# Two row blocks per instruction in the inputs of the second mixer of a two-layer decoder trunk

## The chip, the cores and the metric

The kernel runs on one core of one Trainium2 chip. A core has TensorE (PE, the matrix engine, with its weight loads listed as PEld), VectorE (DVE), ScalarE (ACT) and GpSimd (POOL), which run their own instruction queues in order, and DMA queues that move data between the chip's memory (HBM) and the on-chip memory. The metric is the device time of one execution in microseconds (us); lower is better.

## What is computed

The reference is a trunk of two layers on 16 meta tokens and 256 tokens of width 1024, in float32. Layer 0 is a half-step SwiGLU, attention heads beside gated DeltaNet heads, and another half-step SwiGLU; layer 1 is the same with RWKV-7 time mixing in the middle. The change is in the inputs of that time mixing:

```python
def rwkv7_time_mix(h, mu, w_r, w_k, w_v, w0, w1, w2, a0, a1, a2, g1, g2, k_k, k_a, r_k, ...):
    xx = jnp.pad(h, ((0, 0), (1, 0), (0, 0)))[:, :L] - h          # token differences
    xr, xw, xk, xv, xa, xg = [h + xx * mu[i] for i in range(6)]   # six mixes
    r, k, v = xr @ w_r, xk @ w_k, xv @ w_v
    w_log = -jax.nn.softplus(-(w0 + jnp.tanh(xw @ w1) @ w2)) - 0.5
    a = jax.nn.sigmoid(a0 + (xa @ a1) @ a2)
    g = jax.nn.sigmoid(xg @ g1) @ g2
    kk = l2_normalize((k * k_k).reshape(B_, L, H, N))
    k = k * (1 + (a - 1) * k_a)
    decay = jnp.exp(-jnp.exp(w_log))
    y = rwkv7_recurrence(r, decay, k, v, -kk, kk * a)
    ...
```

## The kernel before

Activations lie transposed: a tile of 128 partitions holds one block of 128 of the 1024 rows (`KD` = 8 blocks), and its T = 272 columns are the tokens. A float32 product is made of three passes of rounded halves (`passes`, lines 216 to 218): every operand is split into a rounding (`h`, made by a cast on ScalarE) and a remainder (`l`, a subtraction on VectorE). Weights go the same way as they are used, 512 columns at a time (`split`, lines 209 and 151).

The time mixing's inputs are made in `TimeMix.inputs`. In order: the low-rank products of the decay, the gate and `a` fill five PSUM banks (`pw`, `pg`); `normed(k)` normalizes block k into `hn` (line 1290) and takes the difference to the token before into `xx`, which lies in the room of `t.hT` (line 1291). `stream(i, s)` makes the mixed input of one of the three large products: per block `mixed` writes `hn + xx * mu` into a tile `mix` (line 1296), line 1304 rounds it into `h`, line 1305 subtracts for `l`. There are three streams: `kx` (key, all made first), `vx` (value) and `rx` (receptance). `joined` (lines 1357 to 1363) forms the low-rank results from two PSUM banks and the token before, by way of a tile `before`. `low_rank` makes the sigmoids of the decay (`ar[:, 1, m]`) and of `a` (`kt[:, m]`), line 1396. `decay(m)` works on block m: a scan along the tokens into `cs` (line 1419), two exponentials (1420, 1421), a copy of five columns into `pc` (1422), the product `bt`, an affine step on `kt` (1424) and the product `kt` with `cs`. The two products are on VectorE for blocks 0 to 3 and on GpSimd for blocks 4 to 7 (`t.tt`, line 151).

Tiles come from the pool `ri`: `mix` and `before` share the tag `mix` with three buffers, `cs` has the tag `low` with four. A tile that finds no free buffer waits until the reader of an older one is done.

`beside` drives the rest: it runs the products of a stream, unit by unit, and takes one step of the given side work after every product of three passes:

```python
beside(units((0, 1), 2, self.key), pairs(low_rank(0, 1, 2, 3)), decays(0, 1))
beside(units((2, 3), 2, self.key), decays(2, 3), sent(0), pairs(chain(low_rank(4, 5, 6, 7), gates())), vx)
beside(units((0, 1), 0, self.value), sent(1), spaced(rx))
beside(units((0, 1), 1, self.receptance), decays(4, 5, 6, 7))
```

A unit's result goes through `key`, `value` or `receptance`, which read the decays' results; `sent(g)` starts the small inverses of a pair of blocks, with DMAs to HBM and back. The program text sets priorities, but a planner orders each engine's instructions by when their inputs and buffers are ready; `after` adds orders by hand (sigmoids and exponentials, which need different activation tables, are kept apart). When the stage ends, `first.close()` gives back the pool `ri`, and the recurrence's tiles (pool `rd`) may take that memory. The recurrence then runs beside the rest of the products (`fills`).

Of the kernel before, what the change touches and what calls it, by code (L numbers as in the profile page):

```python
# [10 lines left out]
F32 = mybir.dt.float32  # L11
F32R = mybir.dt.float32r
AF = mybir.ActivationFunctionType
ALU = mybir.AluOpType
PSUM = bass.MemoryType.PSUM

P = 128
D = 1024
KD = D // P
META = 16  # L20
SEQ = 256
T = META + SEQ
# [6 lines left out]
CH = 64  # L29
# [984 lines left out]
class TimeMix:  # L1014
# [264 lines left out]
    def inputs(self, first):  # L1279

        nc, t, V, ri = self.nc, self.t, self.V, self.ri
        DEC = math.exp(-0.5)
        ar, bt, kt = self.ar, self.bt, self.kt
        hn = self.hn

        xx = t.hT
        ka1 = ri.tile([P, KD], F32, name="ka1")

        def normed(k):
            nc.vector.scalar_tensor_tensor(hn[:, k, 1:], t.hT[:, k, :], self.gain_in[:, k:k + 1], r, ALU.mult, ALU.mult)  # L1290
            nc.vector.tensor_tensor(xx[:, k, :], hn[:, k, 0:T], hn[:, k, 1:], ALU.subtract)

        def mixed(i, k):

            a = ri.tile([P, T + 1], F32, name="mix", tag="mix", bufs=3)[:, :T]
            nc.vector.scalar_tensor_tensor(a, xx[:, k, :], V["mu"][:, KD * i + k:KD * i + k + 1], hn[:, k, 1:], ALU.mult, ALU.add)
            return a

        def stream(i, s):

            h, l = self.x[s]
            for k in range(KD):
                a = mixed(i, k)
                nc.scalar.copy(h[:, k, :], a)
                nc.vector.tensor_tensor(l[:, k, :], a, h[:, k, :].bitcast(F32), ALU.subtract)
                yield

        def pairs(x):
            for _ in x:
# [43 lines left out]
        for k in range(KD):  # L1353
            normed(k)

        def joined(out, now, before, rows):

            n = out.shape[0]
            b = ri.tile([P, T + 1], F32, name="before", tag="mix", bufs=3)[:n]
            nc.gpsimd.memset(b[:, 0:1], 0.0)  # L1360
            nc.vector.tensor_tensor(b[:, 1:], before, r[:n], ALU.mult)
            nc.vector.tensor_tensor(out, now, r[rows], ALU.mult)
            nc.vector.tensor_tensor(out, out, b[:, :T], ALU.add)

        kx = stream(2, 2)
        for _ in range(4):
            next(kx)
        nc.scalar.copy(back[:, 0], self.raw2)
        nc.vector.tensor_tensor(back[:, 1], self.raw2, back[:, 0].bitcast(F32), ALU.subtract)
        mid = self.small("mid")  # L1370
        joined(mid, *pw, slice(0, P))
        nc.scalar.activation(mid[0:64], mid[0:64], AF.Tanh)
        nc.scalar.copy(midh, mid)
        nc.vector.tensor_tensor(midl, mid, midh.bitcast(F32), ALU.subtract)
        for _ in range(4):
            next(kx)
        joined(gmid[0], *pg[:2], slice(0, P))
        joined(gmid[1], pg[2][32:], pg[2][:32], slice(32, 64))
        smask = t.tmp.tile([P, T], F32, name="smask", tag="rstd", bufs=1)
        nc.gpsimd.memset(smask, 1.0)  # L1380
# [6 lines left out]
        def after(which):  # L1387
            stack = ExitStack()
            for x in which:
                stack.enter_context(self.tc.issue_after(x.ins))  # L1390
            return stack
# [22 lines left out]
        def decay(m):  # L1414

            with after(self.sigmoids):
                A, S = kt[:, m], ar[:, 1, m]
                cs = self.decay_tile()
                nc.vector.tensor_tensor_scan(cs, smask, S, 0.0, ALU.mult, ALU.add)
                nc.scalar.activation(S, cs, AF.Exp, scale=-DEC)  # L1420
                self.exps.append(nc.scalar.activation(cs, cs, AF.Exp, scale=DEC))
                nc.scalar.copy(self.pc[:, m, :], S[:, META - 1::CH])
                t.tt(m < 4, bt[:, m], A, cs, ALU.mult)
                nc.scalar.activation(A, A, AF.Identity, scale=V["k_a"][:, m:m + 1], bias=ka1[:, m:m + 1])
                t.tt(m < 4, A, A, cs, ALU.mult)

        self.decay_tile = lambda: ri.tile([P, T], F32, name="cs", tag="low", bufs=4)
        def decays(*ms):
            for m in ms:
                decay(m)  # L1430
                yield

        def sent(g):
            yield
# [5 lines left out]
            yield  # L1440

        vx, rx = stream(3, 0), stream(0, 1)
# [4 lines that stand above are left out]
        self.ready = 0  # L1447
        first.close()
# [431 lines left out]
```

## Time and profile before

| | us |
|---|---|
| median of 3 runs | 1305.07 |
| lowest and highest | 1304.49, 1306.56 |
| the profiled execution | 1305.4 |
| its span in the trace | 1303.7 |
| busy: TensorE, weight loads | 1256.5, 1199.9 |
| busy: VectorE, ScalarE, GpSimd | 901.7, 703.8, 103.6 |

The trace is of the profiled execution. Busy time is the sum of an engine's instructions, overlapping parts counted once. In a timeline a row gives an instruction's start, its duration, engine, line, operation, output and inputs, shapes and count; rows with the same text that follow each other are merged (x2), so their duration is that of all of them together. A list of waits gives who waited for whom, total time, times and the longest. [...]

### The profile page before, as it was taken

What the parts mean: (1) busy time and instruction counts of PE and PEld (TensorE: products, weight loads), DVE (VectorE), ACT (ScalarE), POOL (GpSimd) and SP (SyncE); (2) the same over time, 40 slices, a digit from 0 to 9 for tenths busy, and PEclk for the clock granted to TensorE, in tenths of its full rate; (3) what the DMA queues carried; (4) which work ended last, traced back from release to release, by engine and by line L of the source; (5) the groups of instructions that cost most, each with busy time, mean ns of one, the idle gap of its engine ahead of it and who ended that gap; (6) DMA issues with size and microseconds to landing.
All of it is one profiled execution on the core that took longest, in us unless ns stands there. A gap on an engine that the chain in (4) does not pass through costs nothing.

```text
span 1303.7 us, 28476 instructions
## 1 busy us (share of the span) xinstructions
PE 1256.5 (96%) x11425; PEld 1199.9 (92%) x11425; DVE 901.7 (69%) x1941; ACT 703.8 (54%) x1524; POOL 103.6 (8%) x189
## 2 busy tenths in 40 slices
PE   8999999899999999999999999978999998999997
PEld 8999999788977999999999999967898888999987
DVE  6666666979565866666777766889666677866654
ACT  5555554774455755555555555476444444555553
POOL 2000012002100100000000001103122011000001
PEclk8999999899989999999999999986999999999999
DMA  6545555434112545545656555413432331555652
GB/s 199 188 158 172 167 171 153 128 97 136 40 60 79 185 157 177 194 147 178 190 174 211 170 179 191 132 38 94 128 81 62 111 99 51 167 180 177 206 181 93
DMA packets 199165, 185.72 MB, mean 142 GB/s; under 512 B 28529, under 2 KB 191946, under 8 KB 199034
## 3 DMA queue, kind: packets, MB, share of 16 engines
q1 hardware_dynamic: 198378, 182.78, 44.4%
q8 instruction: 89, 1.46, 0.5%
q10 hardware_dynamic: 656, 1.13, 0.2%
q14 instruction: 42, 0.34, 0.1%
HBM read 180.53 MB, written 3.35 MB: 141 GB/s over the span
## 4 chain that ended last, share of the span: by engine, by line
PE 82%; DVE 9%; ACT 3%; DMA 3%; issue 1%; POOL 1%; SPq 0%; ACTq 0%; DVEq 0%
PE mm L216 22%; PE mm L218 21%; PE mm L217 21%; PE sm L1221 6%; PE mm L979 5%; DVE wl L151 1%; DMA rback<-t 1%; DVE yc L553 1%; PE fx L218 1%; DMA got<-rback 1%; PE fx L216 1%; PE fx L217 1%; ACT wh L209 1%; POOL bt L151 1%; PE fx L913 1%
## 5 line engine op out<-in xcount | busy, mean ns | idle before, releaser
L209 ACT CAST wh<-raw 128x512 fp32r<-128x512 f32 x614 | 372.0, 612 | 385.0 <-PE mm L217 289.8
L151 DVE TENSOR_TENSOR wl<-raw,wh 128x512 fp32r<-128x512 f32 x614 | 416.6, 684 | 222.8 <-ACT wh L209 206.3
L216 PE MATMUL mm<-xh,wh 128*128 128x272 f32 (+1 forms) x1560 | 450.7, 290 | 4.2 <-ACT xh L181 2.3
L218 PE MATMUL mm<-xh,wl 128*128 128x272 f32 (+1 forms) x1560 | 449.8, 289 | 2.4 <-DVE wl L151 2.2
L217 PE MATMUL mm<-xl,wh 128*128 128x272 f32 (+1 forms) x1560 | 448.5, 288 | 0.0
L216 PEld LDWEIGHTS mm<-xh,wh 128*128 128x128 f32 x1560 | 294.6, 189 | 5.9 <-ACT xh L181 2.7
L218 PEld LDWEIGHTS mm<-xh,wl 128*128 128x128 f32 x1560 | 295.5, 190 | 4.3 <-DVE wl L151 3.1
L217 PEld LDWEIGHTS mm<-xl,wh 128*128 128x128 f32 x1560 | 295.5, 190 | 0.8 <-DVE xl L182 0.4
L216 PE MATMUL mm<-hh,wh 128*128 128x272 f32 x528 | 152.4, 289 | 0.0
L217 PE MATMUL mm<-hl,wh 128*128 128x272 f32 x528 | 152.2, 288 | 0.0
L218 PE MATMUL mm<-hh,wl 128*128 128x272 f32 x528 | 151.5, 287 | 0.0
L218 PEld LDWEIGHTS mm<-hh,wl 128*128 128x128 f32 x528 | 99.3, 188 | 0.0
L216 PEld LDWEIGHTS mm<-hh,wh 128*128 128x128 f32 x528 | 99.3, 188 | 0.0
L217 PEld LDWEIGHTS mm<-hl,wh 128*128 128x128 f32 x528 | 99.3, 188 | 0.0
L312 DVE TENSOR_TENSOR hid<-mm,g 128x272 f32<-128x272 f32 (+1 forms) x88 | 38.4, 437 | 18.3 <-PE mm L218 14.8
L309 DVE TENSOR_TENSOR g<-mm,rstd 128x272 f32<-128x272 f32 (+1 forms) x88 | 38.0, 436 | 14.0 <-PE mm L218 12.5
L209 ACT CAST own<-raw 128x512 fp32r<-128x512 f32 (+1 forms) x39 | 24.1, 620 | 42.2 <-PE mm L217 36.7
L979 PE MATMUL mm<-wl,hh 128*128 128x256 f32 (+1 forms) x132 | 42.0, 318 | 0.0
L151 DVE TENSOR_TENSOR own<-raw,own 128x512 fp32r<-128x512 f32 (+1 forms) x39 | 27.1, 700 | 21.4 <-ACT own L209 20.9
L979 PE MATMUL mm<-wh,hl 128*128 128x256 f32 (+1 forms) x132 | 41.9, 317 | 0.0
L979 PE MATMUL mm<-wh,hh 128*128 128x256 f32 (+1 forms) x132 | 41.9, 317 | 0.0
L310 ACT ACTIVATE g<-g 128x272 f32<-128x272 f32 (+1 forms) x88 | 37.2, 428 | 1.5 <-DVE g L309 1.2
(524 smaller groups left out, 2197.1 us busy)
## 6 DMA issues: line engine op xcount, KB each, us to landing
raw<-in_ffn_w_in_dram SPq DMA_DIRECT2D x86, 1024.0 KB
raw<-in_ffn_w_out_dram SPq DMA_DIRECT2D x33, 1024.0 KB
raw<-in_hyb_w_in_dram SPq DMA_DIRECT2D x14, 1024.0 KB
raw<-in_ffn_w_out_dram SPq DMA_DIRECT2D x14, 768.0 KB
raw<-in_hyb_w_out_dram SPq DMA_DIRECT2D x4, 1024.0 KB
raw<-in_rwkv_w_k_dram SPq DMA_DIRECT2D x4, 1024.0 KB
raw<-in_rwkv_w_v_dram SPq DMA_DIRECT2D x4, 1024.0 KB
raw<-in_rwkv_w_r_dram SPq DMA_DIRECT2D x4, 1024.0 KB
```

The lines of the kernel that those rows point to most:

```text
L151: (self.nc.vector if near else self.nc.gpsimd).tensor_tensor(out=out, in0=a, in1=b, op=op)
L209: nc.scalar.copy(wh, raw)
L216: self.nc.tensor.matmul(out, wh, a, start=start, stop=False)
L217: self.nc.tensor.matmul(out, wh, b, start=False, stop=False)
L218: self.last = self.nc.tensor.matmul(out, wl, a, start=False, stop=stop)
L309: nc.vector.tensor_tensor(g[:, :n], pg, r[:, t0:], ALU.mult)
L310: nc.scalar.activation(g[:, :n], g[:, :n], AF.Silu)
L312: nc.vector.tensor_tensor(hid[:, :n], pu, g[:, :n], ALU.mult)
L553: nc.vector.scalar_tensor_tensor(yc, zc[:, j:j + T], cw[:, 12 * j + u:12 * j + u + 1], yc, ALU.mult, ALU.add)
L913: nc.tensor.matmul(pl[:n, :m], qa[:, h, t0:m], ka[:, h, 0:m], start=True, stop=True)
L979: nc.tensor.matmul(po[tt], x[:, k0 + k, tt * P:tt * P + P], w[:, j], start=k0 + k == 0 and x is hh and w is wh, stop=k0 + k == KF - 1 and ...
L1221: self.pace(cost, self.nc.tensor.matmul(out, l, r, start=start, stop=stop))
```

## The change

Token differences are taken for two blocks in one subtraction. A stream makes two mixes, block by block, into one tile of two blocks, and then one cast and one remainder for both. A decay works on two blocks: the scans stay one per block, into the two halves of a `cs` tile of two blocks; the exponentials, the copy and the two products are one instruction for both; the affine step stays one per block, since its scale and bias are per block. The `mix` tiles and the `cs` tiles now share the tag `low` with three buffers of two blocks; `before` has one buffer of its own. A `yield` stands between the scans and the rest of a decay, inside the `with`.

```diff
--- before.py
+++ after.py
@@ -1288,22 +1288,21 @@
 
         def normed(k):
             nc.vector.scalar_tensor_tensor(hn[:, k, 1:], t.hT[:, k, :], self.gain_in[:, k:k + 1], r, ALU.mult, ALU.mult)
-            nc.vector.tensor_tensor(xx[:, k, :], hn[:, k, 0:T], hn[:, k, 1:], ALU.subtract)
-
-        def mixed(i, k):
-
-            a = ri.tile([P, T + 1], F32, name="mix", tag="mix", bufs=3)[:, :T]
-            nc.vector.scalar_tensor_tensor(a, xx[:, k, :], V["mu"][:, KD * i + k:KD * i + k + 1], hn[:, k, 1:], ALU.mult, ALU.add)
-            return a
+            if k % 2:
+                nc.vector.tensor_tensor(xx[:, k - 1:k + 1, :], hn[:, k - 1:k + 1, 0:T], hn[:, k - 1:k + 1, 1:], ALU.subtract)
 
         def stream(i, s):
 
             h, l = self.x[s]
-            for k in range(KD):
-                a = mixed(i, k)
-                nc.scalar.copy(h[:, k, :], a)
-                nc.vector.tensor_tensor(l[:, k, :], a, h[:, k, :].bitcast(F32), ALU.subtract)
-                yield
+            for k in range(0, KD, 2):
+                a = ri.tile([P, 2, T], F32, name="mix", tag="low", bufs=3)
+                for j in range(2):
+                    n = k + j
+                    nc.vector.scalar_tensor_tensor(a[:, j], xx[:, n, :], V["mu"][:, KD * i + n:KD * i + n + 1], hn[:, n, 1:], ALU.mult, ALU.add)
+                    if j:
+                        nc.scalar.copy(h[:, k:k + 2, :], a)
+                        nc.vector.tensor_tensor(l[:, k:k + 2, :], a, h[:, k:k + 2, :].bitcast(F32), ALU.subtract)
+                    yield
 
         def pairs(x):
             for _ in x:
@@ -1356,7 +1355,7 @@
         def joined(out, now, before, rows):
 
             n = out.shape[0]
-            b = ri.tile([P, T + 1], F32, name="before", tag="mix", bufs=3)[:n]
+            b = ri.tile([P, T + 1], F32, name="before", tag="before", bufs=1)[:n]
             nc.gpsimd.memset(b[:, 0:1], 0.0)
             nc.vector.tensor_tensor(b[:, 1:], before, r[:n], ALU.mult)
             nc.vector.tensor_tensor(out, now, r[rows], ALU.mult)
@@ -1414,21 +1413,24 @@
         def decay(m):
 
             with after(self.sigmoids):
-                A, S = kt[:, m], ar[:, 1, m]
-                cs = self.decay_tile()
-                nc.vector.tensor_tensor_scan(cs, smask, S, 0.0, ALU.mult, ALU.add)
+                b = slice(m, m + 2)
+                A, S = kt[:, b], ar[:, 1, b]
+                cs = ri.tile([P, 2, T], F32, name="cs", tag="low", bufs=3)
+                for j in range(2):
+                    nc.vector.tensor_tensor_scan(cs[:, j], smask, S[:, j], 0.0, ALU.mult, ALU.add)
+                yield
                 nc.scalar.activation(S, cs, AF.Exp, scale=-DEC)
                 self.exps.append(nc.scalar.activation(cs, cs, AF.Exp, scale=DEC))
-                nc.scalar.copy(self.pc[:, m, :], S[:, META - 1::CH])
-                t.tt(m < 4, bt[:, m], A, cs, ALU.mult)
-                nc.scalar.activation(A, A, AF.Identity, scale=V["k_a"][:, m:m + 1], bias=ka1[:, m:m + 1])
+                nc.scalar.copy(self.pc[:, b, :], S[:, :, META - 1::CH])
+                t.tt(m < 4, bt[:, b], A, cs, ALU.mult)
+                for j in range(2):
+                    nc.scalar.activation(A[:, j], A[:, j], AF.Identity, scale=V["k_a"][:, m + j:m + j + 1], bias=ka1[:, m + j:m + j + 1])
                 t.tt(m < 4, A, A, cs, ALU.mult)
-
-        self.decay_tile = lambda: ri.tile([P, T], F32, name="cs", tag="low", bufs=4)
+            yield
+
         def decays(*ms):
-            for m in ms:
-                decay(m)
-                yield
+            for m in ms[::2]:
+                yield from decay(m)
 
         def sent(g):
             yield
```

## Rows read from the trace of the kernel before

**Rows 1.** The page's first part: engine, busy us, share of the span, instructions.
```profile
PE 1256.5 (96%) x11425; PEld 1199.9 (92%) x11425; DVE 901.7 (69%) x1941; ACT 703.8 (54%) x1524; POOL 103.6 (8%) x189
```

**Rows 2.** Busy time of each engine by stretch, in the second mixer's inputs.
```profile
core 0: us, PE busy (x) PEld busy (x) DVE busy (x) ACT busy (x) POOL busy (x), PEclk, DMA share, GB/s
...
857.90:862.40 4.50, 1.17 (x24) 1.15 (x25) 4.49 (x16) 4.12 (x13) 0.00 (x0) 1.00 0.26 89
862.40:869.80 7.40, 7.40 (x67) 6.43 (x66) 3.71 (x15) 4.40 (x10) 0.00 (x0) 0.54 0.01 2
...
875.20:879.80 4.60, 1.88 (x10) 1.44 (x11) 4.60 (x14) 4.28 (x11) 0.00 (x0) 0.97 0.26 36
879.80:892.20 12.40, 11.73 (x98) 10.38 (x97) 12.40 (x39) 8.35 (x22) 6.13 (x5) 0.50 0.34 93
892.20:898.00 5.80, 2.56 (x24) 1.73 (x23) 5.36 (x14) 5.01 (x16) 3.47 (x5) 0.50 0.25 42
...
903.40:907.80 4.40, 2.79 (x35) 2.36 (x34) 2.51 (x11) 3.52 (x8) 0.88 (x2) 1.00 0.34 114
907.80:924.00 16.20, 15.93 (x164) 14.00 (x164) 13.13 (x32) 6.05 (x16) 2.00 (x2) 1.00 0.49 133
```

**Rows 3.** Waits in 845 to 912: who waited for whom, us, times, longest.
```profile
POOL am L147 <- DVE mix L1296: 7.4, 1, 7.4
...
PE sm L1469 <- ACT sq L1455: 3.4, 1, 3.4
PE mm L218 <- DVE own L151: 3.2, 3, 1.6
...
PE mm L216 <- DVE l L1305: 2.1, 1, 2.1
...
PE mm L216 <- DVE before L1361: 1.6, 1, 1.6
```

**Rows 4.** VectorE: a merged timeline row, then groups by form (busy us, mean ns).
```profile
837.68 0.79 DVE L1291 TENSOR_TENSOR hT<-hn 128x272 f32<-128x272 f32 x2
...
L1291 DVE TENSOR_TENSOR hT<-hn 128x272 f32<-128x272 f32 x8 | 3.2, 440 | 0.0
...
L1369 DVE TENSOR_TENSOR h<-vtok,h 128x1024 fp32r<-128x1024 f32 x1 | 1.2, 1225 | 0.0
```

**Rows 5.** ScalarE: the same two views.
```profile
850.31 1.06 ACT L1304 CAST h<-mix 128x272 fp32r<-128x272 f32 x3
...
L1304 ACT CAST h<-mix 128x272 fp32r<-128x272 f32 x16 | 6.3, 415 | 4.1 <-DVE mix L1296 4.1
...
L1368 ACT CAST h<-vtok 128x1024 fp32r<-128x1024 f32 x1 | 1.1, 1050 | 4.9 <-PE mm L217 4.9
```

**Rows 6.** The scans among the tile cs's instructions: ns min/median/max, first and last start.
```profile
L1419 DVE TENSOR_TENSOR_SCAN cs<-smask,ar x8: 686/712/724, 854.8 to 875.7; 128x272 f32<-128x272 f32 x8
```

**Rows 7.** Timeline rows of VectorE and one of ScalarE.
```profile
858.39 0.91 DVE L1296 SCALAR_TENSOR_TENSOR mix<-hT,vcols,hn 128x272 f32<-128x272 f32 x2
...
865.31 0.17 DVE L1533 TENSOR_SCALAR dsq<-dsq 128x10 f32<-128x10 f32 x1
...
877.82 0.48 DVE L1296 SCALAR_TENSOR_TENSOR mix<-hT,vcols,hn 128x272 f32<-128x272 f32 x1
...
889.93 0.75 DVE L1533 TENSOR_SCALAR dsq<-dsq 128x10 f32<-128x10 f32 x1
...
895.28 0.79 DVE L1305 TENSOR_TENSOR xl<-mix,xh 128x272 fp32r<-128x272 f32 x1 [0.43 <-ACT xh L1304]
...
906.56 0.43 DVE L1305 TENSOR_TENSOR xl<-mix,xh 128x272 fp32r<-128x272 f32 x1
...
912.89 0.54 ACT L1660 COPY w<-sm 16x128 f32<-16x128 f32 x2 [0.26 <-PE sm L1221]
```

**Rows 8.** GpSimd products of the tiles cs and am (layer 0's), as rows 6.
```profile
L151 POOL TENSOR_TENSOR bt<-kt,cs x4: 758/965/2869, 885.3 to 893.1; 128x272 f32<-128x272 f32 x4
...
L792 POOL TENSOR_TENSOR am<-aq,reordered x6: 1273/1278/2258, 297.0 to 343.6; 128x512 f32<-128x512 f32 x6
```

## The prediction

> **What bounds the kernel now.** The page's first part comes first: TensorE is busy for 1256.5 of 1303.7 us, VectorE for 901.7 [rows 1]. So TensorE sets the time nearly everywhere, and an edit to VectorE or ScalarE work counts only where TensorE stands still for it. The busy times by stretch show that place, the second mixer's inputs from 847.8 to 907.8 us [rows 2]. Within it TensorE does 1.17 of 4.50 us, 1.88 of 4.60 and 2.56 of 5.80, while VectorE is busy for 4.49, 4.60 and 5.36 of the same. From 907.8 on TensorE is busy again for 15.93 of 16.20 us, so I take it that what is saved before 907.8 reaches the end nearly whole. [...] The list of waits then names who ended the idle time [rows 3]: TensorE waited 1.6 us for VectorE's `before` product (which frees a PSUM bank), 3.4 us for ScalarE's `sq` (behind the decays' exponentials), 2.1 us for VectorE's remainder `l` and 3.2 us in three waits for weights' remainders, also VectorE's. The stage is VectorE's, with ScalarE close behind.
>
> **Fixed cost per instruction, VectorE.** Two 128x272 subtractions at line 1291 take 0.79 us together and 0.440 each, so the second adds 0.35 [rows 4]. The 128x1024 subtraction of line 1369 takes 1.225 [rows 4]; (1.225 - 0.440) / 752 columns is 1.04 ns per column. One 544-column instruction then takes 0.440 + 0.284 = 0.724 against 0.79: 0.066 us saved per merger. No row has two blocks of 272, so bounds: at worst nothing is saved, at best the cost is in proportion to the 1024 columns, 1.225 x 544 / 1024 = 0.651, and 0.14 is saved. I take 0.066, the line through both rows. VectorE loses 20 instructions: 4 token differences, 12 remainders, and 4 products `bt` and `kt` of blocks 0 to 3 (blocks 4 to 7 have theirs on GpSimd). 20 x 0.066 = 1.3 us, bounds 0 and 2.8. All of these stand in stretches where VectorE is full, so I count the whole of it.
>
> **ScalarE.** Three casts in a row take 1.06 us, one takes 0.415, so one more adds 0.32; the 1024-column cast takes 1.050, 0.84 ns per column [rows 5]. A 544-column cast is 0.645, against 0.735 for two: 0.09 saved. 12 casts, 8 exponentials and 4 copies of `pc` disappear: 24 x 0.09 = 2.2 us, bounds 0 and, in proportion to the 1024 columns (0.558, so 0.18 saved), 4.2; exponentials and copies are priced as casts. ScalarE has idle time in most of these stretches, so I put this at 0 on the path; its cover is VectorE's own lateness. Where the cover fails, in front of `sq`, four exponentials and two copies become two and one: 0.27 us. Against that, `bt` of block 0 now waits for the exponential of both blocks, one more 0.32; the two cancel.
>
> [...]
>
> **Pairs make the first result later.** TensorE's first product of a stream needed one mix, one cast, one remainder; now it needs two mixes, a cast of 0.645 for 0.415 and a remainder of 0.724 for 0.440: 0.5 us later for cast and remainder alone. The key stream doesn't feel it (its first product waits for `before`, which stands behind the same VectorE queue). The value stream does: its 2.1 us wait for `l` [rows 3] is exposed. The receptance stream starts behind other work.
>
> **The shared buffers.** This is the largest part. `mix` (three buffers) and `cs` (four) become one tag `low` with three double buffers. Each engine's order follows readiness: the scans of blocks 4 to 7 are written after the receptance mixes, yet ran before them; all eight scans lie between 854.8 and 875.7 [rows 6]. With shared buffers I expect the mixes, which are earlier in the program and wait for nothing but a buffer, to take every slot first. Then (a) six instead of three of the value stream's eight mixes run before 870: three ran before 859.3, the last two of them in the row shown, and five from 877.82 on [rows 7]; VectorE has 3.7 us idle in 862.4 to 869.8 [rows 2]. Two mixes take 0.91, one 0.48, so one more is 0.43 and 3 x 0.43 = 1.3 us leave a full stretch. (b) The scans of blocks 4 to 7 move behind the receptance mixes; two of them stand in the full stretch after 875. A scan takes 0.712 [rows 6], less the 0.09 by which neighbours overlap (0.44 against 0.35 above): 0.62, so 1.2 us. (c) The GpSimd products that follow them, from 885.3 on [rows 8], move too. Five VectorE instructions in 889.9 to 896.1 ran long while these ran: the first, over 10 columns, took 0.75 where the same one took 0.17 elsewhere, the last 0.79, where its shape usually takes 0.44 [rows 4, 7]; all five together are 2.4 us over. So VectorE gets 4.9 us lighter between 875 and 898. TensorE can use of that only what it waited: 2.1 for `l`, less the 0.5 for pairs, 1.6 us.
>
> The same 4.9 us come back after 903: four scans are 2.5, the collisions 2.4. VectorE has 1.9 us idle in 903.4 to 907.8 and 3.1 in 907.8 to 924.0 [rows 2], so it just fits; bounds 0 (absorbed) and 1.6 (all that was won). Nearer to absorbed, since TensorE has other products to run there: 0.5. Queued behind a scan that waits for a buffer are remainders of weights and the inverse for blocks 2 and 3; behind the late GpSimd products, the recurrence's masks. Key products of blocks 4 to 7, which read the results, come only among the recurrence's fills. Net gain 1.1, bounds -1.6 and 3.7.
>
> **At nothing.** `before` gets its own single buffer: its memset no longer waits for a mix's release, and the second and third now wait for the first's last reader; they feed only the gates, needed after 862. If that cover went, 0.4 us. The `with` of the decays is now open over one yield; only TensorE's products are issued in between, no ScalarE instruction gets a new place behind the sigmoids; if a cast did, 0.6 us. Steps per loop are the same (two yields per two blocks). No DMA, no weight load and no activation table is added or moved past SP's queue.
>
> **The sum.** 1.3 + 1.1 = 2.4 us. The profiled execution took 1305.4 us with its ends, 0.3 above the median 1305.07; 1305.4 - 2.4 = 1303.0, so 1302.7 on the median's scale. Own range of this case 1300.8 to 1304.4.
>
> **Rivals.**
> *More than that (chance 0.24).* VectorE's relief of 4.9 lets TensorE keep the upper clock after 877, or at least come back to it sooner. Between 879.8 and 892.2 TensorE was busy 11.73 of 12.40 us at 0.50 [rows 2]; at the full clock that work is 5.9 us, and VectorE, full for 12.4, needs 4.9 less. Then the whole relief counts: 1305.1 - 1.3 - 4.9 = 1298.9 us. For it: the fall at 879 follows waits that VectorE ended. Against: casts and sigmoids on ScalarE end at nearly the same time, 4.28 of 4.60 busy.
> *Slower (0.22): the recurrence starts late.* Its masks (GpSimd `am`) waited 7.4 us for the last mix [rows 3], so the recurrence's tiles lie in the memory that this stage gives back, and now the last scan tiles are among what they wait for. The last receptance remainder ended at 907.0 [rows 7]. If scans go only then: first pair 1.3, its two exponentials 1.3, then four GpSimd products of 544 columns. A 272-column one takes 0.758 at least, a 512-column one 1.273 [rows 8], so 544 takes 1.34 and four 5.4, plus an exposed Identity pair of about 1: some 916, and the recurrence's first `w`, at 912.89 [rows 7], comes 3.1 later, or up to 5 if each Identity pair is exposed and the second pair of scans waits its turn. 1305.1 + 3.1 to 5 gives 1308.2 to 1310.1; I take 1308.6. It decides from the point where the last product ends after 912.9, so where the scans start after 904. Against: most slots should be free before.
> [...]
> *No change (0.14).* Only ScalarE and GpSimd are behind TensorE's waits, or the change of order undoes the 1.3: 1305, 1304 to 1306.
>
> **How the numbers follow.** A difference of 0.2%, 2.6 us, is about what a measurement of this kernel can tell: 1302.5 and 1307.7 are the edges. The forecast (0.40) lies across the lower edge: 0.17 faster, 0.23 within. Faster 0.17 + 0.24 = 0.41; within 0.23 + 0.14 = 0.37; slower 0.22. The range 1297.8 to 1309.5 takes in the faster rival and most of the slower one.
>
> **What would show it.** Line 1291 with four 544-column rows near 0.72 us; the scans of blocks 4 to 7 after the receptance mixes, and six value mixes before 870; TensorE's wait for `l` near 0.5 to 1; GpSimd's `bt` after 900. I am wrong if the scans stay near 872 (then only the 1.3 is left), if 544 columns cost as much as two of 272, or if `am` and `w` start later than 915.

## The result, and the profile after

The changed kernel took 1311.27 us in the median (10 runs, 1305.94 to 1324.75); the kernel before, beside it, 1305.61. The ratio is 1.0056, with a 95% interval of 1.0033 to 1.0078: some 6 to 7 us slower. Here and below the ratio is taken over the fast executions of both kernels and is not the quotient of the medians; the two differ by up to 0.0013. The forecast was 2.4 us faster, with a range up to 1309.5; sign and size were wrong. The profiled execution took 1308.96 us (span 1307.2). Its second mixer began 1.0 us earlier than that of before (the reciprocal `rstd` starts at 833.97 for 834.97), so places are compared below by their distance from that row, and the stage up to the end of the span is 473.2 for 468.7 us, 4.5 longer.

Little of it is seen in the engines' totals. The first part of the page, as [rows 1]:

```profile
PE 1255.5 (96%) x11425; PEld 1199.6 (92%) x11425; DVE 901.3 (69%) x1921; ACT 699.5 (54%) x1500; POOL 103.0 (8%) x185
```

The merged instructions cost what was forecast. By line and shape, 834 to 915 us of the changed kernel (busy us, mean ns of one; then the idle time before them):

```profile
L1304 DVE TENSOR_TENSOR l<-mix,h 128x544 fp32r<-128x544 f32 x8 | 5.5, 713 | 0.1
...
L1303 ACT CAST h<-mix 128x544 fp32r<-128x544 f32 x8 | 5.0, 644 | 2.1 <-DVE mix L1301 2.1
...
L1292 DVE TENSOR_TENSOR hT<-hn 128x544 f32<-128x544 f32 x4 | 2.9, 717 | 0.0
```

The order is where it went. The scans of the last four decays stand behind the receptance mixes, the last of which starts at 895.17. VectorE after the change (start, us, engine, line, operation; idle before it and what ended it):

```profile
896.35 0.71 DVE L1420 TENSOR_TENSOR_SCAN cs<-smask,ar 128x272 f32<-128x272 f32 x1
...
899.28 0.71 DVE L1420 TENSOR_TENSOR_SCAN cs<-smask,ar 128x272 f32<-128x272 f32 x1
...
900.01 0.68 DVE L151 TENSOR_TENSOR own<-raw,own 128x512 fp32r<-128x512 f32 x1
...
903.10 0.44 DVE L1501 TENSOR_TENSOR ar<-ar,mm 128x272 f32<-128x272 f32 x1 [0.85 <-PE mm L218]
903.62 1.44 DVE L1503 SCALAR_TENSOR_TENSOR rk<-ar,vcols,kt 128x272 f32<-128x272 f32 x1
904.99 2.16 DVE L399 TENSOR_TENSOR pr<-lay,t 80x512 f32<-80x512 f32 x1
...
916.56 0.44 DVE L1501 TENSOR_TENSOR ar<-ar,mm 128x272 f32<-128x272 f32 x1 [3.44 <-PE mm L218]
```

In the kernel before these four scans had all started by 875.7 [rows 6]. Behind them comes ScalarE (a table load, the exponentials, then `Identity`, which waits for GpSimd's `bt`, then the cast of receptance weights `own`), and then GpSimd. ScalarE after the change, from the two value results on:

```profile
885.09 0.38 ACT L1486 COPY bon<-mm 128x272 f32<-128x272 f32 x1
...
893.50 0.38 ACT L1486 COPY bon<-mm 128x272 f32<-128x272 f32 x1
...
900.29 1.28 ACT L1422 ACT_TABLE_LOAD   x1
901.59 1.20 ACT L1422 ACTIVATE ar<-cs 128x544 f32<-128x544 f32 x2
...
906.30 1.12 ACT L1427 ACTIVATE kt<-kt,ka,vcols 128x272 f32<-128x272 f32 x2 [0.38 <-POOL bt L151]
907.32 0.60 ACT L209 CAST own<-raw 128x512 fp32r<-128x512 f32 x1
```

GpSimd after the change:

```profile
903.41 2.85 POOL L151 TENSOR_TENSOR bt<-kt,cs 128x544 f32<-128x544 f32 x2 [49.66 <-ACT cs L1423]
906.23 5.46 POOL L151 TENSOR_TENSOR kt<-kt,cs 128x544 f32<-128x544 f32 x2
911.65 2.61 POOL L147 TENSOR_TENSOR am<-ab,masks 128x128 f32<-128x128 f32 x3
```

The recurrence's masks `am` (line 147) queue behind four products of 544 columns. And TensorE, which in these rows also serves its queue in order, has the first two of the eight instructions of a product that reads a mask, line 1221 `sm<-tn,am`, between the first passes of receptance block 1. TensorE after the change:

```profile
900.74 0.39 PE L218 MATMUL mm<-xh,own 128*128 128x272 f32 x1 [2.57 <-DVE own L151]
...
907.98 0.60 PE L216 MATMUL mm<-xh,own 128*128 128x272 f32 x1 [1.13 <-ACT own L209]
...
909.45 0.39 PE L1221 MATMUL sm<-w,got 16*16 16x64 f32 x2 [0.65 <-ACT w L1662]
913.49 0.47 PE L1221 MATMUL sm<-tn,am 64*64 64x64 f32 x2 [3.65 <-POOL am L147]
913.89 0.59 PE L218 MATMUL mm<-xh,own 128*128 128x272 f32 x1
```

The rest of receptance block 1 is issued only behind these two, at 913.89, and then at a granted clock of 0.50 (913.9 to 916.0). The busy times by stretch (columns as in [rows 2]; PEclk is the clock granted to TensorE, as a share of the full one):

```profile
875.20:879.80 4.60, 4.18 (x73) 3.48 (x73) 4.45 (x13) 2.74 (x6) 0.00 (x0) 0.72 0.29 45
879.80:892.20 12.40, 10.06 (x61) 9.18 (x62) 12.40 (x40) 3.43 (x6) 0.00 (x0) 0.69 0.21 25
...
907.80:916.00 8.20, 3.72 (x15) 3.02 (x16) 5.28 (x8) 1.94 (x6) 6.46 (x5) 0.51 0.45 96
916.00:924.00 8.00, 8.00 (x86) 7.13 (x85) 4.55 (x12) 2.99 (x8) 0.86 (x2) 0.86 0.56 187
```

So there was a relief, and a large one. From 875.2 to 879.8 TensorE was busy for 4.18 us where it had been 1.88 [rows 2]. The copies of the two value blocks' results stand 51.1 and 59.5 us behind the stage's start (885.09 and 893.50), in the kernel before 57.8 and 68.4 (892.72 and 903.39): 6.6 and 8.9 us were won. The first receptance block's product (903.10, before 909.81) still stands 5.7 better. The second (916.56, before 912.53) stands 5.0 worse. Between the two the changed kernel lost 10.7 us. TensorE's waits in that stretch, 0.65 for `w`, 1.13 for ScalarE's `own`, 3.65 for `am` and a small one of 0.17, are 5.6 of it; 18 products that come 0.23 us apart (0.50 granted from 901.3 to 904.5), where they come 0.13 apart at 1.00 (896.0 to 897.9), are 1.8; and small products that came behind block 1 before and now come ahead of it (from 905.21 to 906.85, and the pairs at 909.45 and 913.49), 2.4. Together that is 9.8 of the 10.7.

### The profile page after: what moved, and what is told of

It reads as the page before. It is cut to its first block, busy times and chain, and to the rows that moved or that the text cites. A ratio compares the mean times of both kernels' runs of the same rounds, so it can differ in the third digit from the quotient of the medians.

```text
span 1307.2 us, 28425 instructions
## 1 busy us (share of the span) xinstructions
PE 1255.5 (96%) x11425; PEld 1199.6 (92%) x11425; DVE 901.3 (69%) x1921; ACT 699.5 (54%) x1500; POOL 103.0 (8%) x185
## 3 DMA queue, kind: packets, MB, share of 16 engines
q10 hardware_dynamic: 656, 1.13, 0.2%
## 4 chain that ended last, share of the span: by engine, by line
PE 83%; DVE 8%; ACT 3%; DMA 2%; issue 2%; POOL 1%; SPq 0%; DVEq 0%; POOLq 0%; ACTq 0%
PE mm L216 22%; PE mm L218 21%; PE mm L217 21%; PE sm L1221 6%; PE mm L979 5%; DVE wl L151 1%; PE fx L218 1%; PE fx L216 1%; PE fx L217 1%; PE fx L913 1%; DMA raw<-in_ffn_w_in_dram 0%; DMA rback<-t 0%; PE gd L420 0%; PE fx L933 0%; PE gd L432 0%
```

## The theories, and a measure for the runs

**L (late decays).** The buffers shared by mixes and scans push the last four decays behind the receptance mixes; from there the delay runs through in-order queues to `am` and TensorE. **G (grain).** Instructions over two blocks bring the first results later. **P (GpSimd's grain).** A GpSimd product of 544 columns holds up VectorE longer than two of 272. In all runs everything is computed. Beside the ratio to the kernel before, the table gives the distance from the stage's start (reciprocal `rstd`) to the second receptance product and to the end of the span; single profiles differ by a few us, the ratios decide.

| kernel | ratio (95% interval) | to second receptance product | to end of span |
|---|---|---|---|
| before | 1 | 77.6 | 468.7 |
| changed kernel | 1.0056 (1.0033 to 1.0078) | 82.6 | 473.2 |
| e2: before, late scans | 1.0070 (1.0045 to 1.0095) | 83.3 | 478.2 |
| e3: before, paired decays | 0.9995 (0.9979 to 1.0011) | 77.6 | 471.0 |
| e4c: before, paired streams | 0.9973 (0.9953 to 0.9994) | 74.5 | 469.0 |
| e5: changed, decays before receptance mixes | 0.9986 (0.9971 to 1.0001) | 78.4 | 467.8 |
| e6: changed, GpSimd in single blocks | 1.0050 (1.0029 to 1.0071) | 82.1 | 475.8 |
| e8: changed, late products on VectorE | 0.9998 (0.9976 to 1.0020) | 79.6 | 471.0 |
| e9: changed, first masks on VectorE | 1.0012 (0.9992 to 1.0032) | 79.5 | 468.8 |
| e10: changed, decays behind sigmoids | 0.9998 (0.9981 to 1.0016) | 78.4 | 469.0 |
| e11: changed, TensorE's order alone | 1.0026 (1.0013 to 1.0040) | 79.4 | 469.5 |
| e12: e4c with decays before receptance mixes | 0.9977 (0.9959 to 0.9995) | 73.4 | 464.8 |

## The experiments: which part of the change loses

**Late scans alone (e2).** The kernel before, every instruction over one block, with the scan tiles of blocks 4 to 7 put under the mixes' tag:

```diff
-                cs = self.decay_tile()
+                cs = self.decay_tile() if m < 4 else ri.tile([P, T + 1], F32, name="cs", tag="mix", bufs=3)[:, :T]
```

> The kernel before, one block per instruction everywhere; only the scan tiles of blocks 4 to 7 take their buffers from the mixes' tag, so that they have to stand behind the receptance mixes. Theory L (the shared buffers make the last four decays late): slower than the kernel before by 3 to 6 us; the four scans after 895 us in the span, GpSimd's bt after 900, TensorE waits 2 us or more for GpSimd's am or its clock falls between 905 and 920. Theory G (two-block instructions bring the first results later): no change, within 1.3 us. Theory P (a 544-column product on GpSimd holds VectorE twice as long): little of the loss, under 2 us, since the products stay at 272 columns.

Measured 1314.88 us, ratio 1.007: the loss of the change and more (9.5 us by the medians, where 3 to 6 were expected), without a single merged instruction. GpSimd:

```profile
910.65 2.61 POOL L151 TENSOR_TENSOR bt<-kt,cs 128x272 f32<-128x272 f32 x2 [54.37 <-ACT cs L1421]
...
922.54 1.72 POOL L147 TENSOR_TENSOR am<-ab,masks 128x128 f32<-128x128 f32 x3
```

The scans ran from 908.4 on, the masks behind the products from 922.54 on. Sharing buffers is enough for a loss. The road is another one, though: here receptance block 1 is through before a mask is read, and behind it TensorE waits 1.8 us for `w` and 1.1 for `am`, where 2 or more were expected, or a fallen clock (it was granted 0.99 from 900 to 908, 0.80 from 908 to 916 and 0.63 from 916 to 924). So e2 shows that late scans lose; it does not show through which queue the changed kernel loses.

**Paired decays alone (e3)**, in two double buffers of their own; the rest as before:

```diff
+                cs = ri.tile([P, 2, T], F32, name="cs", tag="low", bufs=2)
+                for j in range(2):
+                    nc.vector.tensor_tensor_scan(cs[:, j], smask, S[:, j], 0.0, ALU.mult, ALU.add)
...
-                t.tt(m < 4, bt[:, m], A, cs, ALU.mult)
+                t.tt(m < 4, bt[:, b], A, cs, ALU.mult)
```

> Only the decays work on two blocks, with two cs buffers of their own (the room that four single ones had); mixes, remainders, token differences as before. Theory L: scans of blocks 4 to 7 stay near 872 us, so no loss: within 2 us of the kernel before (4 mergers on VectorE are 0.3 us). Theory G: slower by 2 us or more, since bt of a block waits for both exponentials. Theory P: slower by 1 to 3 us, with VectorE rows over 1 us near 885 to 895.

Measured 1304.32 us, 0.9995: no difference. Its last scan starts at 878.7, GpSimd's products of 544 columns at 881.5, and TensorE waits nowhere for `am`. Products of that length are no loss where they come early.

**Paired token differences and streams alone (e4c)**, the decays over one block, in three buffers that they share with `before`:

```diff
-            a = ri.tile([P, T + 1], F32, name="mix", tag="mix", bufs=3)[:, :T]
...
+                a = ri.tile([P, 2, T], F32, name="mix", tag="mix", bufs=2)
...
-        self.decay_tile = lambda: ri.tile([P, T], F32, name="cs", tag="low", bufs=4)
+        self.decay_tile = lambda: ri.tile([P, T + 1], F32, name="cs", tag="cs", bufs=3)[:, :T]
```

> Only the streams and the token differences work on two blocks (two mix buffers of two blocks); the decays are as before, one block each, with three cs buffers of their own that the tile 'before' shares. Theory L: no loss, between 2 us faster (16 mergers of 0.066 are 1.1 us) and 1.5 us slower. Theory G: slower by 2 us or more, with a longer wait of TensorE for l and xl. Theory P: as L, GpSimd's products are single.

Measured 1302.21 us, 0.9973: faster than both kernels. That is against G, which expected a loss of 2 us or more from the pairs. One decay is late here too; there are three buffers for the decays instead of four:

```profile
903.74 2.00 POOL L151 TENSOR_TENSOR bt<-kt,cs 128x272 f32<-128x272 f32 x1 [15.29 <-ACT cs L1420]
906.46 1.26 POOL L151 TENSOR_TENSOR kt<-kt,cs 128x272 f32<-128x272 f32 x1 [0.73 <-ACT kt L1423]
907.69 3.93 POOL L147 TENSOR_TENSOR am<-ab,masks 128x128 f32<-128x128 f32 x4
```

One late block instead of four sets the masks only to 907.69, and TensorE doesn't wait for them.

**The changed kernel with early decays (e5).** Only their place in the program differs:

```diff
-        beside(units((0, 1), 0, self.value), sent(1), spaced(rx))
-        beside(units((0, 1), 1, self.receptance), decays(4, 5, 6, 7))
+        beside(units((0, 1), 0, self.value), sent(1), decays(4, 5, 6, 7), spaced(rx))
+        beside(units((0, 1), 1, self.receptance))
```

> The changed kernel, with the decays of blocks 4 to 7 written ahead of the receptance mixes (third beside instead of fourth), so that they come first for the shared buffers. Theory L: most of the loss comes back: within 2 us of the kernel before; GpSimd's bt before 895, TensorE's wait for am gone. Theory G and theory P: the loss of some 5 us stays, since all two-block instructions are still there.

Measured 1303.44 us, 0.9986. GpSimd's products now start at 886.96, the masks at 894.33:

```profile
886.96 4.78 POOL L151 TENSOR_TENSOR bt<-kt,cs 128x544 f32<-128x544 f32 x2 [37.19 <-ACT cs L1423]
891.70 2.67 POOL L151 TENSOR_TENSOR kt<-kt,cs 128x544 f32<-128x544 f32 x2
894.33 0.65 POOL L147 TENSOR_TENSOR am<-ab,masks 128x128 f32<-128x128 f32 x1
```

All merged instructions and the shared buffers are kept; two lines in another place take back the loss. Together, e2 and e5 show L: it is the place of four decays that loses.

## The experiments: which queue carries it

**GpSimd's products over one block again (e6)**, eight of 272 columns, as late as in the changed kernel:

```diff
-                t.tt(m < 4, bt[:, b], A, cs, ALU.mult)
+                halves = lambda *xs: [[x] if m < 4 else [x[:, 0], x[:, 1]] for x in xs]
+                for o, x, y in zip(*halves(bt[:, b], A, cs)):
+                    t.tt(m < 4, o, x, y, ALU.mult)
```

> The changed kernel, in which only GpSimd's products bt and kt of blocks 4 to 7 are again instructions of one block (eight of 272 columns for four of 544). Everything is computed; the last four scans stay late. L (the shared buffers make the last four decays late, and the masks queue behind their products on GpSimd): nothing comes back, since eight products of 272 take as long as four of 544 in sum; the ratio to the kernel before stays at 1.003 to 1.008, and TensorE's wait for am stays at 2 to 5 us. P (a product of 544 columns on GpSimd holds VectorE's SBUF accesses for twice as long as one of 272): at least half of the loss comes back, ratio 1.002 or less, and the slow VectorE rows after 903 (1.44 for rk, 2.16 for pr) become those of before the change (0.49, 1.01) or at most half way.

Measured 1312.79 us, 1.005: the loss stays. On VectorE there is something in P:

```profile
903.01 0.49 DVE L1506 SCALAR_TENSOR_TENSOR rk<-ar,vcols,kt 128x272 f32<-128x272 f32 x1
903.42 1.59 DVE L399 TENSOR_TENSOR pr<-lay,t 80x512 f32<-80x512 f32 x1
```

`pr` took 1.59, half way between the 2.16 beside products of 544 columns and the 1.04 that its line takes in the median of the changed kernel. That brings nothing back, since GpSimd is no sooner done: its eight products took 9.54 us (6.04 for `bt`, 3.50 for `kt`), the four of the changed kernel 8.31. TensorE now waits longer for ScalarE's cast of `own`, which runs behind `bt` and `Identity`, than for `am` (waits from 835 on: total, times, longest):

```profile
PE mm L216 <- ACT own L209: 5.0, 1, 5.0
...
PE sm L1221 <- POOL am L147: 2.0, 1, 2.0
```

**The late products on VectorE (e8).** GpSimd's queue holds nothing ahead of the masks; the scans stay late.

```diff
-                t.tt(m < 4, bt[:, b], A, cs, ALU.mult)
+                t.tt(True, bt[:, b], A, cs, ALU.mult)
...
-                t.tt(m < 4, A, A, cs, ALU.mult)
+                t.tt(True, A, A, cs, ALU.mult)
```

> The changed kernel with bt and kt of blocks 4 to 7 on VectorE instead of GpSimd; all is computed, the scans of blocks 4 to 7 stay late (near 897), and GpSimd's queue holds nothing ahead of the masks am. L with the loss going through GpSimd's queue: the products take 4 x 0.72 us on VectorE instead of some 12 us of GpSimd's time, am starts within 3 us after the last mix has been read, no TensorE wait for am above 1 us, and most of the loss comes back: 1303 to 1307, ratio 0.998 to 1.002. L with the loss going through the scans' own lateness (VectorE's and ScalarE's order after 896): the loss stays or grows, since VectorE gets 2.9 us more to do in that stretch: ratio 1.004 to 1.009.

Measured 1307.47 us, 0.9998 (the kernel before, beside it, 1306.01): the loss is gone, though VectorE has four instructions more and the scans start as late. So the scans' lateness itself, and ScalarE's exponentials behind it, are not the cost. The cost is in what goes through GpSimd: the products, which take 8.31 us there in the changed kernel (some 12 were expected), and what queues behind them.

**The first masks on VectorE (e9)**, the late products left on GpSimd:

```diff
-        self.t.pool_tt(am, self.ab[g][:, c - 1], self.masks[:, l:l + 1].broadcast_to([P, 2, CH]), ALU.mult)
+        self.t.tt((g, c) in ((0, 1), (0, 2), (1, 1)), am, self.ab[g][:, c - 1], self.masks[:, l:l + 1].broadcast_to([P, 2, CH]), ALU.mult)
```

> The changed kernel with the first three masks am of the recurrence on VectorE instead of GpSimd; all is computed. GpSimd's late products and their collisions with VectorE stay as they are. If the loss is that am queues behind the late products on GpSimd: the wait of 3.6 us of TensorE for am goes, the receptance products of block 1 start near 912 instead of 913.9 (3.6 us and what the clock lost in 907.8 to 916), ratio 0.998 to 1.002. If the loss is the collisions of VectorE with GpSimd after 903 (some 3 us of long rows): it stays, ratio 1.004 to 1.008, and TensorE waits for VectorE in place of GpSimd.

Measured 1306.70 us, 1.0012: most of it is back, while the collisions stay (`pr` 2.17, `kt` on GpSimd 6.02 for two). So the collisions' cost on VectorE is not the loss. But the masks are hardly earlier: on VectorE they start 76.7 us behind the stage's start, for 77.7 in the changed kernel. First VectorE's row, then TensorE's:

```profile
911.00 0.68 DVE L151 TENSOR_TENSOR am<-ab,masks 128x128 f32<-128x128 f32 x3
```

```profile
911.12 0.59 PE L218 MATMUL mm<-xh,own 128*128 128x272 f32 x1 [0.66 <-DVE own L151]
...
914.01 0.69 PE L1221 MATMUL sm<-tn,am 64*64 64x64 f32 x8
```

What changed is the place of `sm<-tn,am` on TensorE: all eight instructions stand behind receptance block 1, so nothing waits for a mask in front of it.

**TensorE's order alone (e11).** In e8, as in e9, the early `sm<-tn,am` stood behind receptance block 1. Here only that is written; the masks stay on GpSimd and late:

```diff
-        self.each(p, (am, tn))
+        with ExitStack() as stack:
+            if (g, c) == (0, 1):
+                stack.enter_context(self.tc.issue_after(self.t.last.ins))
+            self.each(p, (am, tn))
```

> The changed kernel in which only TensorE's order differs: the one early product of the recurrence that reads a mask (sm<-tn,am, line 1221), which stands between receptance blocks 0 and 1, is queued behind block 1. This is TensorE's order also in the kernel with the first masks on VectorE and in the one with the late products on VectorE; here everything stays on GpSimd, as late as in the changed kernel. All is computed. If the loss is that TensorE's in-order queue stands behind a late mask: receptance block 1 begins by 912, the wait for am goes or falls below 1 us, and the ratio is 0.999 to 1.003, as with the masks on VectorE (1.0012). If the loss is the lateness of the masks itself, that is of the recurrence that follows from them, or GpSimd's collisions with VectorE: the wait for am moves behind block 1 but the loss stays, ratio 1.004 to 1.007.

Measured 1308.87 us, 1.0026 (the kernel before, beside it, 1305.06). The masks start as late as in the changed kernel, 77.8 us behind the stage's start for 77.7, and no wait for them is left on TensorE. The planner moved one thing more: six of the products `sm<-w,got`, for two, stand ahead of the rest of block 1, as in e9. First GpSimd's rows, then TensorE's:

```profile
904.22 4.31 POOL L151 TENSOR_TENSOR bt<-kt,cs 128x544 f32<-128x544 f32 x2 [48.98 <-ACT cs L1423]
...
913.27 1.74 POOL L147 TENSOR_TENSOR am<-ab,masks 128x128 f32<-128x128 f32 x3
```

```profile
910.25 0.40 PE L216 MATMUL mm<-xh,own 128*128 128x272 f32 x1 [3.81 <-ACT own L209]
...
912.16 0.60 PE L218 MATMUL mm<-xh,own 128*128 128x272 f32 x1 [0.66 <-DVE own L151]
...
915.04 0.69 PE L1221 MATMUL sm<-tn,am 64*64 64x64 f32 x8
```

Block 1 goes on 76.7 us behind the stage's start (912.16 - 835.46), for 79.9 in the changed kernel. The ratio lies at the upper end of the first expectation: about half of 0.0056 comes back with TensorE's order, the rest not, and the intervals of e11 and of the changed kernel just overlap. What remains shows in TensorE's first row: it waits 3.81 us for `own`, which ScalarE casts only behind the `Identity` that waits for GpSimd's `bt`. Those two `bt` took 4.31 us beside `pr`, where two such products took 2.62 in e10 from 877.12 on, with VectorE idle until 881.11, so the collisions are part of this wait. The same wait of 3.81 stands in e9, and in e8, where the cast ran ahead of the `Identity` pair, there is none, but one of 2.9 for `w`. That this wait is the rest of the loss is argued from these rows; the intervals of e8, e9 and e11 overlap and don't show it.

## The experiments: a better place

**Decays straight behind the sigmoids (e10)**, ahead of the value stream:

```diff
-        beside(units((2, 3), 2, self.key), decays(2, 3), sent(0), pairs(chain(low_rank(4, 5, 6, 7), gates())), vx)
+        beside(units((2, 3), 2, self.key), decays(2, 3), sent(0), pairs(chain(low_rank(4, 5, 6, 7), gates())), decays(4, 5, 6, 7), vx)
```

> The changed kernel with the decays of blocks 4 to 7 written straight behind the sigmoids, so that their scans take buffers of the shared tag ahead of the value stream's last mixes, and before all receptance mixes; all is computed. L: scans of blocks 4 to 7 by 880, GpSimd's products by 897, no wait for am, and as fast as the version with the decays written between value and receptance stream (0.9986) or 1 us faster: ratio 0.996 to 0.999. If instead lateness of the first results (G) is what costs, the value stream's products come later than in the changed kernel, a wait of 2 us or more for its remainder l or for own shows before 890, and the ratio is 1.001 or more.

Measured 1306.18 us, 0.9998: a miss. The scans ran by 876, the first mask at 882.3, but two waits took the gain. TensorE's longest waits and a row of VectorE:

```profile
PE sm L1471 <- ACT sq L1457: 7.7, 2, 6.0
PE mm L218 <- DVE bon L151: 4.0, 2, 3.4
```

```profile
881.11 2.17 DVE L1301 SCALAR_TENSOR_TENSOR mix<-hT,vcols,hn 128x272 f32<-128x272 f32 x2 [4.49 <-POOL kt L151]
```

`sq` of a key block stands on ScalarE behind all of the decays' exponentials and `Identity` instructions, and the value mixes wait 4.49 us for the buffers that GpSimd's products hold. The same shared buffers, taken from the other side: now the mixes queue behind the decays.

**The streams' pairs with the decays early (e12)**, e4c with the two lines of e5.

> Token differences and streams for two blocks at a time in buffers of their own, decays one block at a time in three buffers of their own (the version that ran at 0.9973), and now the decays of blocks 4 to 7 written ahead of the receptance mixes. All is computed. L: the last decay, which in that version still went to 904, runs before 895, GpSimd is free of its products by 900, nothing else gets later: ratio 0.995 to 0.998. If the pairs alone are what gains (VectorE's and ScalarE's saved fixed cost) and the last block's place costs nothing: the same 0.997. If scans ahead of the receptance mixes now delay TensorE's products: ratio 0.999 or more.

Measured 1301.84 us, 0.9977; e4c had 0.9973. The last `bt` on GpSimd is 11 us earlier (58.6 us behind the stage's start for 69.7), and the time doesn't follow: in neither does TensorE wait for `am`, so the late decay of e4c cost nothing that could be measured. These two are the fastest versions, some 3 us faster than the kernel before.

## Why the prediction was wrong, step by step

**Fixed cost on VectorE: right, but small.** 544 columns were put at 0.724 us and took 0.713 to 0.717. 1.3 us for 20 mergers stands by these rows, though VectorE's busy time fell only from 901.7 to 901.3, collisions included; e4c, with 16 of them, gained 3.5 us (0.27% of 1305.38), so more than this, and from what else was not tried.

**ScalarE: too small in busy time.** A 544-column cast was put at 0.645 and took 0.644. Busy time fell from 703.8 [rows 1] to 699.5, so 4.3 us for 24 instructions fewer, 0.18 each, where the spacing of casts in a row had given me 0.09: most of these instructions don't stand in a row, and alone two take 0.83 [rows 5]. Whether any of it reached the end no run shows, since none merges on ScalarE alone.

**Pairs make the first result later: not seen.** TensorE's wait for `l` (2.1 in [rows 3]) is gone, and both value results came earlier.

**The shared buffers: the order was right, the sizes were not.** The scans of blocks 4 to 7 moved behind the receptance mixes as forecast. Four value mixes started before 870 and six before 874, not six before 870. The relief was put at 4.9 us of VectorE's work, of which TensorE could use 1.6; TensorE was 6.6 and 8.9 us earlier at the two value results. The mis-sized term is the use: it had only the wait for `l`, and the clock is missing from it. After being busy for 4.18 of 4.60 us, where it had been idle for most of it, TensorE was granted 0.69 instead of 0.50 in the 12.4 us that follow. That is what the rival "more than that" expected; that the one brought the other is not shown. What made the relief is open: in e2, where the same scans are late without a pair, the two value results stand at 61.9 and 67.8 (57.8 and 68.4 before), so late scans alone give none; in e5, with pairs and early decays, they stand at 49.9 and 66.4.

**The step that failed** is "The same 4.9 us come back after 903 ... so it just fits; bounds 0 (absorbed) and 1.6 (all that was won)", of which 0.5 was taken. It counted VectorE's idle time, and VectorE was not what the late decays burdened. They are a chain over four in-order queues: scans on VectorE (with the remainder `own` behind them, a wait of 2.57 on TensorE), a table load and exponentials on ScalarE, `bt` on GpSimd, `Identity` on ScalarE (with the cast of `own` behind it), `kt` and then `am` on GpSimd, and `sm<-tn,am` on TensorE with receptance block 1 behind it. From the last receptance mix at 895.17 to the end of the masks at 914.26 that takes 19 us, and the masks are needed at 909.8. The prediction named "behind the late GpSimd products, the recurrence's masks" in that very place and gave it no price there. Measured in its place: 10.7 us between the two receptance products, for 0.5. The range did not allow for it either: the prediction's own bounds, 0 to 2.8 and -1.6 to 3.7, give 1298.6 to 1306.7 from its 1305.1, not the stated 1300.8 to 1304.4, and the measured time lies above both.

**"No activation table is ... moved": wrong.** The load of 1.28 us moved with the first late exponential, from 879.28 to 900.29, into the chain.

**The rival "slower" had the right mechanism** and a price of 3 to 5 us; 4.5 us by the profiles and 5.7 by the medians came out. It was wrong on where the price falls. It saw the recurrence's first `w` (forecast 916 to 918, measured 909.16, no later than before when the stage's start is taken off: 75.2 for 77.9) and made the late end of the last product, after 912.9, the condition. The products ended at 911.7, and it was lost all the same, since the one to wait was not `w` but the receptance pass queued behind a product with `am`. That its price nearly fits is in part luck.

**The collisions.** `rk` and `pr` on VectorE were over by 0.95 and 1.1 us (1.44 for 0.49, 2.16 for 1.04), and e9 shows a `pr` as long with most of the loss gone. But GpSimd paid the more of it, and that side the prediction left out: its four products took 8.31 us where they take 5.24 by e10 (two `bt` in 2.62 beside an idle VectorE), 3.1 more, just ahead of the masks that TensorE waited 3.65 for. No run has these products late on GpSimd with VectorE idle beside them, so how much of the loss the collisions are stays open.

## What to carry to other kernels

Two kinds of tiles under one tag are a statement about order: whoever is earlier in the program takes the buffers, and the other's whole chain moves behind it. Follow that chain over every in-order queue to the first instruction of the bounding engine that reads from it, and see what stands behind that one in its queue; idle time of one engine says nothing about it. Where the saved memory is wanted, write the work whose results are needed first ahead in the program: here two lines in another place were worth 0.7%.

## What the runs showed of the hardware

In these rows VectorE and GpSimd took longer side by side: a GpSimd product of 544 columns, 1.31 us with VectorE idle (two for 2.62 in e10), took 3.0 with VectorE at work (two for 6.02 in e9), and `rk` and `pr` of VectorE, beside such products in the changed kernel, took 0.95 and 1.1 us more than the medians of their lines there (0.49 and 1.04); beside products of 272 columns `pr` took 0.55 more (1.59 in e6). And around the wait for `am` TensorE was both half idle and slow: in those 8.2 us (907.8 to 916.0) it was busy for 3.72 at a granted clock of 0.51, and behind the wait, at 0.50, products came 0.23 us apart that come 0.13 apart at 1.00 (896.0 to 897.9).
